# A two-layer trunk on one core: each engine's order tied to the order of the trace, forgetting heads spread over their group, all their probabilities transposed by DMA

## The chip, the cores and the metric

The kernel runs on one core of one Trainium2 chip. TensorE (PE in the profile) multiplies matrices, VectorE (DVE) and ScalarE (ACT) do the elementwise work, GpSimd (POOL) a little of it, and SyncE (SP) issues nearly all transfers. The metric is the device time of one execution in microseconds, as the median of several; less is better. Instructions on one engine run in the order in which they stand in its queue; between engines, semaphores make an instruction wait for what it reads or overwrites.

## The reference

Two layers on a sequence of 256 tokens with 2048 channels. Layer 0 mixes tokens by forgetting attention (16 heads of 128), layer 1 by dilated sliding windows (8 heads in 3 groups, values 256 wide). Each mixer is followed by an MLP with squared ReLU and 8192 hidden channels. All in fp32.

```python
def fox_attention(h, w_in, b_f, q_gain, k_gain, w_out):
    q, k, v, f = jnp.split(h @ w_in, [H * dh, 2 * H * dh, 3 * H * dh], axis=-1)
    q = rms_norm(q.reshape(B, S, H, dh), q_gain)
    k = rms_norm(k.reshape(B, S, H, dh), k_gain)
    c = jnp.cumsum(jax.nn.log_sigmoid(f + b_f), axis=1)
    # per block of 128 query tokens, every head
    s = jnp.einsum('bqhd,bkhd->bhqk', q_i, k) * scale
    s = s + jnp.transpose(c_i, (0, 2, 1))[..., None] - c_keys[:, :, None, :]
    p = jax.nn.softmax(jnp.where(causal, s, -jnp.inf), axis=-1)
    return jnp.einsum('bhqk,bkhd->bqhd', p, v) ... @ w_out

def reference(x, ...):
    for i in range(2):
        h = rms_norm(x, mix_norm_g[i])
        x = x + (fox_attention if i == 0 else dilated_attention)(h, ...)
        h = rms_norm(x, mlp_norm_g[i])
        x = x + sq_relu_mlp(h, mlp_w_up[i], mlp_w_down[i])
    return x
```

## The kernel before, in words

**Products.** All weights are read once from HBM, in an order fixed by a list (`plan`). A chunk is 256 rows by 512 columns (512 KB). `load` brings it into one of five raw buffers through SP's queue. `split` (L302) cuts it into a high part (`wh`, a cast on ACT, L312) and a low part (`wl`, raw minus high on DVE, L313), with five buffers of each. PE multiplies high by high, high by low and low by high, so that the sum is close to fp32. A k-step covers 128 rows of the weights: for each of two token blocks three matmuls of 512 columns (L347 to L349). A chunk lasts two k-steps. After every second k-step `split` is called for the chunk that is five ahead, since one pair of buffers has just come free, and `load` for the raw chunk whose buffer that split frees.

**Ticks.** After each k-step `product_steps` calls `jobs.tick()`. `Jobs` holds generators ("jobs"): a job is run until it yields a number (so many ticks to wait) or a key (wait until some other job has put it into `done`). Everything beside the products is such a job: the norms of queries and keys (`qk_chain`), values (`v_chain`), attention heads, additions to the residual stream. So the place at which an instruction is traced is set by these yields.

**From trace to queue.** The traced instructions are then put in order by a list scheduler of the compiler's, engine by engine. It keeps dependencies, and a few more ties written by hand: `behind(...)` keeps the instructions in it after given ones. In `move`, a DMA stands behind the latest weight load; in `fox_head`, `pv` and `dil_head` the small matmuls stand behind the latest product; in `p_split` and `qk_chain` casts and subtractions stand behind the latest chunk's cast and cut. Besides these ties the scheduler may move an instruction ahead of others traced before it or behind others traced after it.

**Forgetting heads.** The stage makes four groups `j` of four heads. For each, three products of 16 k-steps: queries (`fq`), keys (`fk`), values (`fv`). A group takes 48 ticks; its heads run in the ticks of its last products and of the next group's first. After a product of queries or keys, `qk_chain` norms it, transposes it through DRAM by DMA, and makes two halves of tokens (t = 0, 1) two ticks apart, each scaled and cut in high and low on ACT and DVE; with the second half the key ("fk", j) is done. The first head's scores come two ticks later.

`fox_head` (L739) makes one head:
- the bias row, from DRAM to all partitions (`bias`, 192 KB, through SP, two buffers), four ticks later the mask is added to it (L752, DVE);
- scores on PE (`sc_f`, L666 to L669), for two blocks of 128 queries, then on DVE scores plus bias (`s_f`, L765) and the row maximum (`nm_f`, L768);
- one tick later exp on ACT with the row sums (L771); one tick later on DVE the reciprocal (L774) and the scaling (L776);
- the transposition of the probabilities, in `p_turned` (L613): a 32 by 32 transpose on DVE (L617), four block moves to DRAM (`pblocks`, 48 KB each, SP), four ticks later one read back (`turned`, 192 KB, SP), and five ticks after it `p_split` (L627) makes the high part on ACT (`pTh`, L632) and the low on DVE (`pTl`, L634). In the last group, heads 14 and 15 use `p_transposed` (L637) instead: three PE transposes and copies on ACT and DVE;
- three ticks later `pv` (L597), the product with the values on PE (`po_f`, L606, L607), cut into the operands of the output projection (`oTfh` on ACT, L609; `oTfl` on DVE, L610).

The offset `at` (L741) says how many ticks after ("fk", j) a head's scores come: 2, 6, 10, 14 for the heads of groups 0 to 2; 2, 4, 6, 9 in group 3. The first head asks for its bias early and waits for the keys; the others ask for it `at` - 4 ticks after the keys.

**What follows.** The output projection takes its 16 steps in two parts (`in_pair`): steps 0 to 11 of two column blocks, then 12 to 15 of each, so that heads 12 to 15 are needed 24 ticks after its start. Then the first MLP, the dilated layer with its `dil_head` jobs (of the same kind, three scores each), its projection, and the second MLP. `dilation_tables` makes three tables of 128 by 384 with about 28 short DVE operations; it is spawned after the output projection is traced.

Of the kernel before, what the change touches and what calls it, by code (L numbers as in the profile page):

```python
# [42 lines left out]
class Jobs:  # L43
# [5 lines left out]
    def __init__(self):  # L49
        self.now = 0  # L50
        self.live = []
        self.done = set()
        self.running = False

    def spawn(self, gen):
        self.live.append([self.now, None, gen])
        if not self.running:
            self._run()
# [18 lines left out]
    def tick(self):  # L77
        self.now += 1
        self._run()

    def need(self, key):
        tries = 0
        while key not in self.done:
            self.tick()
            tries += 1
            assert tries < 10000, key
# [3 lines left out]
def trunk(ctx: ExitStack, tc, x, fox_w_in, fox_b_f, fox_q_gain, fox_k_gain, fox_w_out, dil_w_in,  # L90
          dil_q_gain, dil_k_gain, dil_w_out, mix_norm_g, mlp_norm_g, mlp_w_up, mlp_w_down, out):
    nc = tc.nc
    jobs = Jobs()

    const = ctx.enter_context(tc.tile_pool(name="const", bufs=1))
    act = ctx.enter_context(tc.tile_pool(name="act", bufs=1))
# [516 lines left out]
    def p_turned(p, name):  # L613


        turned = work.tile([P, 4, 3, 32], F32, tag="s", name=f"turned_{name}", bufs=S_BUFS)
        nc.vector.transpose(turned.rearrange("p j b r -> p b j r"), p.rearrange("p (b j c) -> p b j c", b=3, c=32))  # L617
        blocks = dram.tile([4, 32, 4, 3 * 32], F32, tag="pblocks", name=f"pblocks_{name}", bufs=4)
        for i in range(4):
            move(blocks[:, :, i, :].rearrange("j c x -> c j x"),  # L620
                 turned[32 * i:32 * i + 32].rearrange("p j b r -> p j (b r)"))
        yield 4
        move(turned.rearrange("p i b r -> p (i b r)"), blocks.rearrange("j c i x -> (j c) (i x)"))
        yield 5
        return turned
# [11 lines left out]
    def p_transposed(p, name):  # L637

        pt = ps_tp.tile([P, 3 * P], F32, tag="tp", name=f"ptp_{name}")
        for b in range(3):  # L640
            nc.tensor.transpose(pt[:, b * P:(b + 1) * P], p[:, b * P:(b + 1) * P], ident)
        p_hi, p_lo = (work.tile([P, S], F32R, tag=f"pT{x}", name=f"pT{x}_{name}", bufs=2) for x in "hl")
        p_whole = work.tile([P, P], F32, tag="s", name=f"pTw_{name}", bufs=S_BUFS)
        nc.scalar.copy(p_hi, pt[:, 0:S])
        nc.vector.tensor_sub(p_lo, pt[:, 0:S], p_hi.bitcast(F32))
        nc.scalar.copy(p_whole, pt[:, S:3 * P])
        return p_hi, p_lo, p_whole
# [90 lines left out]

    def fox_head(j, hh, qT, kT, vt):  # L739
        h = 4 * j + hh  # L740
        at = ((0, 2, 4, 7) if j == 3 else (0, 4, 8, 12))[hh] + 2  # L741
        yield ("fq", j)
        yield "gate"
        yield "mask"
        if hh:
            yield ("fk", j)
            yield at - 4

        bias = work.tile([P, 3 * P], F32, tag="bias", name=f"bias{h}", bufs=2)
        move(bias, negc[h:h + 1, :].to_broadcast([P, 3 * P]))  # L750
        yield 4
        nc.vector.tensor_add(bias, bias, tables["mask"])  # L752
        if hh == 0:
            yield ("fk", j)
            yield 2
        ps = ps_sc.tile([P, 512], F32, tag="sc", name=f"sc_f{h}")
        with behind(issued["product"]):
            for t in range(NT):
                scores(ps, t, qT[hh // 2], kT[hh // 2], hh % 2)
        s = work.tile([P, 3 * P], F32, tag="s", name=f"s_f{h}", bufs=S_BUFS)  # L760
        nm = small.tile([P, NT], F32, tag="nm", name=f"nm_f{h}")
        den = small.tile([P, NT], F32, tag="den", name=f"den_f{h}")
        spans = [slice(0, P), slice(P, 3 * P)]
        for t in range(NT):
            nc.vector.scalar_tensor_tensor(s[:, spans[t]], ps[:, spans[t]], c_q[:, t, h:h + 1],  # L765
                                           bias[:, spans[t]], ALU.add, ALU.add)
        for t in range(NT):
            nc.vector.tensor_reduce(nm[:, t:t + 1], s[:, spans[t]], AX.X, ALU.max, negate=True)  # L768
        yield 1
        for t in range(NT):  # L770
            nc.scalar.activation(s[:, spans[t]], s[:, spans[t]], AF.Exp, bias=nm[:, t:t + 1],  # L771
                                 accum_out=den[:, t:t + 1])
        yield 1
        nc.vector.reciprocal(den, den)  # L774
        for t in range(NT):
            nc.vector.tensor_scalar_mul(s[:, spans[t]], s[:, spans[t]], den[:, t:t + 1])  # L776
        if j == 3 and hh > 1:
            yield 2
            pt_sb = p_transposed(s, f"f{h}")
            yield 1  # L780
        else:
            turned = yield from p_turned(s, f"f{h}")
            yield ("fv", j)
            pt_sb = p_split(turned, f"f{h}")
        yield 3
        if ("f", h // 2) not in oT:
            oT["f", h // 2] = tuple(
                act.tile([P, 2, S], F32R, tag=f"aT{x}", name=f"oTf{x}_{h}", bufs=KC // 2) for x in "hl")
        hi, lo = oT["f", h // 2]
        yield from pv(pt_sb, vt, [hh * P], [hi[:, h % 2, :]], [lo[:, h % 2, :]], f"f{h}")  # L790
        jobs.done.add(("of", h))


    def dil_head(q4, i, qTs, kTs, vt):
        h = 2 * q4 + i
        for g in range(3):
            yield ("dqk", q4, g)
        yield (3 if q4 == 3 else 6) * i + 2
        s = work.tile([P, 3, 3 * P], F32, tag="sd", name=f"sd{h}", bufs=1)
        for g in range(3):  # L800
            yield ("table", g)
            ps = ps_sc.tile([P, 512], F32, tag="sc", name=f"sc_d{h}_{g}")
            with behind(issued["product"]):
                for t in range(NT):
                    scores(ps, t, qTs[g], kTs[g], i)
            slope = 2.0 ** (-8.0 * (g * DH + h + 1) / N_SLOPES)
            nc.vector.scalar_tensor_tensor(s[:, g, :], tables[g], -slope, ps[:, 0:3 * P], ALU.mult, ALU.add)
            yield 1
        nm = small.tile([P, NT], F32, tag="nm", name=f"nm_d{h}")
        den = small.tile([P, NT], F32, tag="den", name=f"den_d{h}")  # L810
        spans = [slice(0, P), slice(P, 3 * P)]
        for t in range(NT):
            nc.vector.tensor_reduce(nm[:, t:t + 1], s[:, :, spans[t]], AX.XY, ALU.max, negate=True)
        yield 1
        for t in range(NT):
            nc.scalar.activation(s[:, :, spans[t]], s[:, :, spans[t]], AF.Exp, bias=nm[:, t:t + 1],
                                 accum_out=den[:, t:t + 1])
        yield 1
        nc.vector.reciprocal(den, den)
        p = work.tile([P, 3 * P], F32, tag="s", name=f"p_d{h}", bufs=S_BUFS)  # L820
        nc.vector.tensor_add(p, s[:, 0, :], s[:, 1, :])
        nc.vector.tensor_add(p, p, s[:, 2, :])
        for t in range(NT):
            nc.vector.tensor_scalar_mul(p[:, spans[t]], p[:, spans[t]], den[:, t:t + 1])
        if (q4, i) == (3, 1):
            yield 2
            pt_sb = p_transposed(p, f"d{h}")
        else:
            turned = yield from p_turned(p, f"d{h}")
            yield ("dv", q4)  # L830
            pt_sb = p_split(turned, f"d{h}")
        yield 3
        hi, lo = (act.tile([P, 2, S], F32R, tag=f"aT{x}", name=f"oTd{x}_{h}", bufs=KC // 2) for x in "hl")
        oT["d", h] = hi, lo
        yield from pv(pt_sb, vt, [i * S, i * S + P], [hi[:, 0, :], hi[:, 1, :]], [lo[:, 0, :], lo[:, 1, :]], f"d{h}")
        jobs.done.add(("od", h))
# [147 lines left out]

    tag = "n0"
    for j in range(4):
        qT = [heads_pair(f"fqT{j}_{i}", i, False) for i in range(2)]
        kT = [heads_pair(f"fkT{j}_{i}", 3 + i, True) for i in range(2)]
        vt = values(f"fv{j}")
        product(keys_h(tag), lhs_h(tag), lambda acc: qk_chain(  # L990
            acc, tag, ("fq", j), [(0, 2, FOX_G, qT[0]), (2 * P, 2, FOX_G, qT[1])]))
        if j == 0:
            jobs.need("wf")
            gate(tag)
        product(keys_h(tag), lhs_h(tag), lambda acc: qk_chain(
            acc, tag, ("fk", j), [(0, 2, FOX_G + 1, kT[0]), (2 * P, 2, FOX_G + 1, kT[1])]))

        for hh in range(4):
            jobs.spawn(fox_head(j, hh, qT, kT, vt))
        product(keys_h(tag), lhs_h(tag), lambda acc: v_chain(acc, tag, ("fv", j), vt))  # L1000
# [42 lines left out]
```

## Time and profile before

| | before |
|---|---|
| three executions | 2166.27, 2163.27, 2166.0 us |
| median | 2166.0 us |
| the profiled execution | 2165.23 us |
| its span, first to last instruction | 2163.5 us |
| mean granted clock of PE | 0.999 |
| PE, DVE, ACT busy share of the span | 99%, 65%, 51% |

The profile is one execution. The forgetting stage runs from about 30 to 330 us, the first MLP to about 1150, the dilated stage to about 1430, the second MLP to the end. In a line of the timeline stand the start, the duration, the engine, the source line, the operation, output and inputs, and in brackets how long the engine was idle before it and what released it. In the groups, "xN" is a count and three durations are the least, the median and the greatest in ns. In the view of waits stand the engine and its instruction, whom it waited for, the total, how many times, and the longest. Matmuls are pipelined: a 512-column one shows 0.38 us, but they start every 0.216 us.

### The profile page before, as it was taken

What the parts mean: (1) busy time and instruction counts of PE and PEld (TensorE: products, weight loads), DVE (VectorE), ACT (ScalarE), POOL (GpSimd) and SP (SyncE); (2) the same over time, 40 slices, a digit from 0 to 9 for tenths busy, and PEclk for the clock granted to TensorE, in tenths of its full rate; (3) what the DMA queues carried; (4) which work ended last, traced back from release to release, by engine and by line L of the source; (5) the groups of instructions that cost most, each with busy time, mean ns of one, the idle gap of its engine ahead of it and who ended that gap; (6) DMA issues with size and microseconds to landing.
All of it is one profiled execution on the core that took longest, in us unless ns stands there. A gap on an engine that the chain in (4) does not pass through costs nothing.

```text
span 2163.5 us, 29880 instructions
## 1 busy us (share of the span) xinstructions
PE 2145.4 (99%) x11129; PEld 1904.4 (88%) x11129; DVE 1409.8 (65%) x1890; ACT 1101.6 (51%) x1524; POOL 41.6 (2%) x40
## 2 busy tenths in 40 slices
PE   9999999999999999999999999999999999999999
PEld 7888888998998998998887888888988988988988
DVE  6778778765665565566668778676755655655664
ACT  6555565644444454455555555545544543544542
POOL 0000000000000000000000000000000000000000
PEclk9999999999999999999999999999999999999999
DMA  7877687766666666667777776758656656656664
GB/s 240 253 240 232 218 274 262 236 202 202 201 204 204 200 201 204 203 200 241 243 239 222 226 243 212 259 198 272 204 203 201 201 204 204 199 203 203 202 212 141
DMA packets 312369, 470.77 MB, mean 218 GB/s; under 512 B 34648, under 2 KB 121888, under 8 KB 312224
## 3 DMA queue, kind: packets, MB, share of 16 engines
q1 hardware_dynamic: 311632, 468.20, 66.8%
q8 instruction: 87, 1.43, 0.3%
q10 hardware_dynamic: 560, 0.66, 0.1%
q14 instruction: 58, 0.48, 0.1%
q0 software_dynamic: 32, 0.02, 0.0%
HBM read 445.76 MB, written 23.03 MB: 217 GB/s over the span
## 4 chain that ended last, share of the span: by engine, by line
PE 89%; DVE 3%; issue 1%; ACT 0%; DMA 0%; POOL 0%; SPq 0%; ACTq 0%; DVEq 0%; POOLq 0%
PE acc L347 19%; PE acc L349 19%; PE acc L348 19%; PE up_n1a_acc L411 5%; PE up_n3a_acc L411 5%; PE up_n1a_sc L411 3%; PE up_n1a_tp L411 3%; PE up_n3a_sc L411 3%; PE up_n3a_tp L411 3%; PE up_n3a_acc L415 3%; PE up_n1a_acc L415 3%; DVE wl L313 1%; PE up_n3a_tp L415 1%; PE up_n3a_sc L415 1%; PE up_n1a_tp L415 1%; PE up_n1a_sc L415 1%
## 5 line engine op out<-in xcount | busy, mean ns | idle before, releaser
L313 DVE TENSOR_TENSOR wl<-raw,wh 128x1024 fp32r<-128x1024 f32 (+1 forms) x801 | 973.8, 1220 | 632.7 <-ACT wh L312 629.3
L312 ACT CAST wh<-raw 128x1024 fp32r<-128x1024 f32 (+1 forms) x801 | 836.5, 1047 | 901.8 <-PE acc L349 553.7
L348 PE MATMUL acc<-wl,hT_n 128*128 128x512 f32 x896 | 341.8, 381 | 1.3 <-DVE wl L313 1.1
L347 PE MATMUL acc<-wh,hT_n 128*128 128x512 f32 x896 | 342.6, 384 | 0.0
L349 PE MATMUL acc<-wh,hT_n 128*128 128x512 f32 x896 | 340.8, 381 | 0.0
L347 PE MATMUL acc<-wh,aTh_n1a 128*128 128x512 f32 x512 | 194.0, 379 | 0.0
L348 PE MATMUL acc<-wl,aTh_n1a 128*128 128x512 f32 x512 | 194.0, 379 | 0.0
L349 PE MATMUL acc<-wh,aTl_n1a 128*128 128x512 f32 x512 | 194.0, 379 | 0.0
L348 PEld LDWEIGHTS acc<-wl,hT_n 128*128 128x128 f32 x896 | 170.3, 190 | 24.8 <-DVE wl L313 2.3
L349 PEld LDWEIGHTS acc<-wh,hT_n 128*128 128x128 f32 x896 | 170.2, 190 | 23.7
L347 PEld LDWEIGHTS acc<-wh,hT_n 128*128 128x128 f32 x896 | 170.2, 190 | 23.2 <-ACT wh L312 0.4
L347 PE MATMUL acc<-wh,aTh_n3a 128*128 128x512 f32 x480 | 181.9, 379 | 0.0
L348 PE MATMUL acc<-wl,aTh_n3a 128*128 128x512 f32 x480 | 181.9, 379 | 0.0
L349 PE MATMUL acc<-wh,aTl_n3a 128*128 128x512 f32 x480 | 181.9, 379 | 0.0
L411 PE MATMUL up_n1a_acc<-hT_n,wh 128*128 128x512 f32 x512 | 181.6, 382 | 0.0
L411 PE MATMUL up_n3a_acc<-hT_n,wh 128*128 128x512 f32 x512 | 181.6, 382 | 0.0
L415 PE MATMUL up_n3a_acc<-hT_n,wl 128*128 128x256 f32 x512 | 139.6, 273 | 0.0
L415 PE MATMUL up_n1a_acc<-hT_n,wl 128*128 128x256 f32 x512 | 139.6, 273 | 0.0
L348 PEld LDWEIGHTS acc<-wl,aTh_n1a 128*128 128x128 f32 x512 | 96.8, 189 | 13.8
L349 PEld LDWEIGHTS acc<-wh,aTl_n1a 128*128 128x128 f32 x512 | 96.8, 189 | 13.7
L347 PEld LDWEIGHTS acc<-wh,aTh_n1a 128*128 128x128 f32 x512 | 96.8, 189 | 13.6
L411 PEld LDWEIGHTS up_n3a_acc<-hT_n,wh 128*128 128x128 f32 x512 | 96.8, 189 | 13.5
(687 smaller groups left out, 3156.6 us busy)
## 6 DMA issues: line engine op xcount, KB each, us to landing
raw<-in_mlp_w_up_dram SPq DMA_DIRECT2D x256, 512.0 KB, 4.3
raw<-in_mlp_w_down_dram SPq DMA_DIRECT2D x256, 512.0 KB, 3.7
raw<-in_dil_w_in_dram SPq DMA_DIRECT2D x192, 256.0 KB, 4.0
raw<-in_fox_w_in_dram SPq DMA_DIRECT2D x95, 512.0 KB, 5.5
raw<-in_fox_w_out_dram SPq DMA_DIRECT2D x32, 512.0 KB, 5.1
raw<-in_dil_w_in_dram SPq DMA_DIRECT2D x32, 512.0 KB, 5.0
raw<-in_dil_w_out_dram SPq DMA_DIRECT2D x32, 512.0 KB, 4.0
blocks_n<-turned_n SPq DMA_DIRECT2D x96, 64.0 KB, 3.2
```

Of the source, the lines that this page charges most:

```text
L312: issued["cast"] = nc.scalar.copy(hi[:, part, :], raw[:, part, :])
L313: issued["cut"] = nc.vector.tensor_sub(lo[:, part, :], raw[:, part, :], hi[:, part, :].bitcast(F32))
L347: nc.tensor.matmul(acc[t], ah[:, tok], hi, start=first, stop=False)
L348: nc.tensor.matmul(acc[t], ah[:, tok], lo, start=False, stop=False)
L349: issued["product"] = nc.tensor.matmul(acc[t], al[:, tok], hi, start=False, stop=last)
L411: issued["product"] = nc.tensor.matmul(banks[b], hi[:, i, col], in_turn(tokens.rearrange("p x s -> p (x s)"), P // 2), start=first, stop=last)
L415: nc.tensor.matmul(banks[b][:, 0:S], lo[:, i, col], in_turn(tokens[:, 0, :], P // 2), start=False, stop=False)
```

## The change

One hook is added to `Jobs`, which runs after every tick. From tick 24 on it runs `pin`, which goes over all instructions traced since the last call and adds to each a dependency on the instruction traced before it on the same engine. The dependency is of a kind that orders and needs no semaphore, so that the scheduler keeps every engine's queue in traced order. The offsets of the heads in groups 0 to 2 become 2, 8, 20, 26 (group 3 keeps 2, 4, 6, 9). Heads 14 and 15 go through `p_turned` and `p_split` like the others, and in the last group `pv` comes two ticks after the split instead of three. In the dilated stage's last group the second head starts five ticks behind the first instead of three.

```diff
@@ class Jobs
+        self.each_step = lambda: None
@@ tick
         self.now += 1
         self._run()
+        self.each_step()
@@ trunk
+    pinned = {"last": None}
+
+    def pin():
+
+        traced = nc.cur_bb.bb.instructions
+        at = len(traced)
+        while at and traced[at - 1] is not pinned["last"]:
+            at -= 1
+        if pinned["last"] is None:
+            at = len(traced)
+        for i in traced[at:]:
+            before = pinned.get(i.engine)
+            if before is not None:
+                tc.add_manual_dep(
+                    i, before.name,
+                    mybir.DependencyInfo(mybir.DependencyClass.NoSync, mybir.DependencyReason.DATA),
+                    reason="in the order of the trace")
+            pinned[i.engine] = i
+        pinned["last"] = traced[-1]
@@ fox_head
-        at = ((0, 2, 4, 7) if j == 3 else (0, 4, 8, 12))[hh] + 2
+        at = ((2, 4, 6, 9) if j == 3 else (2, 8, 20, 26))[hh]
...
-        if j == 3 and hh > 1:
-            yield 2
-            pt_sb = p_transposed(s, f"f{h}")
-            yield 1
-        else:
-            turned = yield from p_turned(s, f"f{h}")
-            yield ("fv", j)
-            pt_sb = p_split(turned, f"f{h}")
-        yield 3
+        turned = yield from p_turned(s, f"f{h}")
+        yield ("fv", j)
+        pt_sb = p_split(turned, f"f{h}")
+        yield 2 if j == 3 else 3
@@ dil_head
-        yield (3 if q4 == 3 else 6) * i + 2
+        yield (5 if q4 == 3 else 6) * i + 2
@@ the four groups of forgetting heads
     for j in range(4):
+        if j == 0:
+            jobs.each_step = lambda: jobs.now >= 24 and pin()
```

## The prediction

> **What bounds the kernel now.** The page's first part is read first, then four stretches side by side (the columns: the stretch and its length, busy us and instructions of PE, weight loads, DVE, ACT, POOL, then the granted clock, the DMA share, GB/s).
>
> ```profile
> PE 2145.4 (99%) x11129; PEld 1904.4 (88%) x11129; DVE 1409.8 (65%) x1890; ACT 1101.6 (51%) x1524; POOL 41.6 (2%) x40
> 30.00:330.00 300.00, 294.92 (x1444) 254.51 (x1443) 229.43 (x419) 173.85 (x301) 15.24 (x11) 1.00 0.75 242
> 330.00:1150.00 820.00, 820.00 (x4295) 732.82 (x4294) 518.41 (x631) 407.16 (x530) 6.30 (x5) 1.00 0.66 214
> 1150.00:1430.00 280.00, 275.39 (x1348) 240.79 (x1347) 210.41 (x318) 159.68 (x243) 16.83 (x9) 0.99 0.72 231
> 1430.00:2159.00 729.00, 729.00 (x3928) 654.55 (x3927) 434.16 (x491) 343.64 (x425) 0.70 (x1) 1.00 0.63 205
> ```
>
> TensorE is the bound: it idles for nothing in either MLP, 300 - 294.9 = 5.1 us in the forgetting stage, 280 - 275.4 = 4.6 us in the dilated one. What PE waits for longest in those two stages:
>
> ```profile
> PE sc_d L666 <- DVE sd L807: 2.3, 2, 2.0
> PE po_f L606 <- DVE s_f L765: 1.9, 1, 1.9
> PE po_d L606 <- DVE pTl_d L634: 1.8, 1, 1.8
> PE po_f L606 <- ACT pTh_f L632: 0.9, 1, 0.9
> ```
>
> So the change can win at most about 10 us by order, while each wait that a fixed order makes is a full loss. The clock of the work is the tick, one k-step of six 512-column products; ACT casts one weight chunk per two ticks:
>
> ```profile
> 1140.06 1.05 ACT L312 CAST wh<-raw 128x1024 fp32r<-128x1024 f32 x1 [1.54 <-PE acc L349]
> 1147.83 1.05 ACT L312 CAST wh<-raw 128x1024 fp32r<-128x1024 f32 x1 [1.54 <-PE acc L349]
> ```
>
> (1147.83 - 1140.06) / 6 = 1.295 us a tick. Each cast starts when PE has left a buffer (the releaser): in traced order ACT and DVE cannot run ahead of PE, and what is traced behind a chunk's cast and cut waits for both. The first forgetting head in the trace of before:
>
> ```profile
> 87.48 0.38 PE L666 MATMUL sc_f<-fkT_0w,fqT_0w 128*128 128x128 f32 x2
> 107.49 0.42 DVE L634 TENSOR_TENSOR pTl_f<-turned_f,pTh_f 128x256 fp32r<-128x256 f32 x1
> 108.52 0.27 PE L606 MATMUL po_f<-pTh_f,fv0h 128*128 128x256 f32 x1
> ```
>
> From its scores to its last operand (107.49 + 0.42) are 20.4 us, and its values product ran 21.0 us after the scores. In traced order that product stands 14 ticks behind them, plus two score groups of other heads (some 0.5 us each): due at 14 x 1.295 + 1.0 = 19.1 us. The scheduler of before had moved it two ticks back.
>
> **The change part by part.** *The pin.* It adds no instruction and no semaphore; it fixes each engine's order to the traced one. In both MLPs the orders of before and after hardly differ: 0, hidden by PE's 100% there; the ring holds five chunks, ten ticks or 13 us ahead. One move into the first MLP counts: about 28 operations for the dilation tables go from the output projection to its start.
>
> ```profile
> L209 DVE TENSOR_TENSOR dist<-dist,ok 128x384 f32<-128x384 f32 x1 | 0.6, 553 | 0.0
> ```
>
> 28 x 0.45 = 12.6 us of DVE in eight ticks, beside four cuts of 1.22 us: DVE falls back at most 7 us, under the 13 us lead. Cost 0; without cover up to 7. The dilated stage keeps its order but for a few moves by one or two ticks: 0, between -4.6 (its idle) and +4.
>
> *The forgetting heads, groups 0 to 2.* Offsets 8, 20, 26 put head 1's scores 6 ticks behind head 0's, head 3's 6 behind head 2's. On SP head 1's bias request now stands behind head 0's four block moves (before: ahead of them), likewise head 3's behind head 2's. Rows for a walk:
>
> ```profile
> 88.92 0.74 DVE L765 SCALAR_TENSOR_TENSOR s_f<-sc_f,c_q,bias 128x128 f32<-128x128 f32 x2 [0.25 <-PE sc_f L669]
> 89.58 1.22 DVE L313 TENSOR_TENSOR wl<-raw,wh 128x1024 fp32r<-128x1024 f32 x1
> 90.71 0.60 DVE L768 TENSOR_REDUCE nm_f<-s_f 128x1 f32<-128x128 f32 x2
> 91.02 0.40 ACT L771 ACTIVATE s_f<-s_f,nm_f 128x128 f32<-128x128 f32 x1 [1.88 <-DVE nm_f L768]
> 91.91 1.03 ACT L312 CAST wh<-raw 128x1024 fp32r<-128x1024 f32 x1
> 92.04 0.17 DVE L774 RECIPROCAL den_f<-den_f 128x2 f32<-128x2 f32 x1 [0.73 <-ACT s_f L771]
> 92.83 0.58 DVE L617 STREAM_TRANSPOSE turned_f<-s_f 128x384 f32<-128x384 f32 x1
> 94.96 1.94 SPq L269 DMA_DIRECT2D pblocks_f<-turned_f  x4
> L752 DVE TENSOR_TENSOR bias<-bias,mask x16: 513/548/559, 80.1 to 317.6; 128x384 f32<-128x384 f32 x16
> DMA to landing us min/median/max: 3.3/4.2/5.6
> pblocks_f<-turned_f SPq DMA_DIRECT2D x56, 48.0 KB, 2.1
> turned_f<-pblocks_f SPq DMA_DIRECT2D x14, 192.0 KB, 5.5
> L632 ACT CAST pTh_f<-turned_f x14: 388/397/408, 106.6 to 326.5; 128x256 fp32r<-128x256 f32 x14
> ```
>
> From the start of head 0's scores: cast to 1.25, cut to 2.5, scores add and maximum (0.74, 0.60) to 3.85, four exp instructions (91.02 to 91.91) to 4.9, next cast to 5.95 and cut to 7.2, since the traced order has them ahead of the reciprocal; reciprocal to transpose (92.04 to 93.4) to 8.6; four moves to 10.4. Then bias 1 is requested: 10.4 + 4.2 = 14.6, and DVE, in order, stands at its mask add till then. Mask add, scores, maximum to 16.5; exp 17.55; cast and cut 19.8; reciprocal to transpose 21.2; cut 22.4; and only then, as DVE's order has it, head 0's last operand (0.42) at 22.8. Due 19.1: **3.6 us**. Head 1: transposed at 21.2, four moves to 23.0, landed at 25.1 (2.1), read back at 30.6 (5.5), split at 31.4 (0.40, 0.42); due 20 ticks and three groups behind head 0's scores, shifted by the wait: 25.9 + 1.5 + 3.6 = 31.0. **0.4**.
>
> Head 2's product comes out later, for two more things stand ahead of its last operand: a projection output's cut and the next projection's sums of squares.
>
> ```profile
> L610 DVE TENSOR_TENSOR oTfl<-po_f,oTfh 128x256 fp32r<-128x256 f32 x16 | 6.5, 413 | 11.0 <-ACT oTfh L609 10.9
> L532 DVE TENSOR_REDUCE ss_('fk', 1)_1429<-sq_('fk', 1)_1_1427 128x4 f32<-128x512 f32 x1 | 0.7, 686 | 0.0
> ```
>
> 22.8 + 0.4 + 1.55 (two sums and a short scaling, taken as the reciprocal's 0.17) = 24.8, against 19.1: 5.7; and ACT may stand at head 1's split till its read has landed, 0 to 2.4 us: half, 1.2. Bias 3 and head 3 hold it as bias 1 and head 1 hold head 0's. Halves of the 1.2 may fall together with DVE's, so 5.7 + 0.6 = **6.3**. The first scores wait for the keys' second half, whose operations stand behind two casts, the first half and both value copies on ACT:
>
> ```profile
> 83.45 0.50 ACT L567 ACTIVATE fkT_0w<-qn_('fk', 0)_0_766,gain 128x256 f32<-128x256 f32 x1
> 85.12 0.69 ACT L586 ACTIVATE fv0w<-acc,rstd_n 128x512 f32<-128x512 f32 x1
> 86.63 0.91 ACT L567 ACTIVATE sq_('fk', 0)_0_715<-qn_('fk', 0)_1_769,gain 128x256 f32<-128x256 f32 x2
> 87.91 0.42 DVE L576 TENSOR_TENSOR fkT_0l<-sq_('fk', 0)_0_715,fkT_0h 128x256 fp32r<-128x256 f32 x1
> ```
>
> Counted from four ticks (5.2 us) before the scores: 2 x 1.05 + 4 x 0.5 + 2 x 0.69 + 0.91 + 2 x 0.42 = 7.2, less some 0.5 by overlap: **1.5** late. Last, a long wait costs the clock:
>
> ```profile
> 1159.00:1162.00 3.00, 1.13 (x6) 0.64 (x4) 3.00 (x6) 1.04 (x1) 0.00 (x0) 1.00 0.66 201
> 1162.00:1166.00 4.00, 3.83 (x13) 3.23 (x14) 3.51 (x6) 0.00 (x0) 0.00 (x0) 0.59 0.62 159
> ```
>
> After one wait of about 2 us PE ran the next 4 us at 0.59: 4 x 0.41 = **1.7** lost, taken once a group. The Trainium skill, TensorE: Matmul & The Clock Gate, Part 1, has the rate halved only after an idle window of about 3.4 us; the row differs, as a shorter wait did it, and by the page's rule the sum would be some 5 us less.
>
> A group: 1.5 + 3.6 + 0.4 + 6.3 + 1.7 = 13.5; three: 40.5.
>
> *Group 3.* Heads 14 and 15 go by DMA: eight moves, two reads and two transposes more, six PE transposes less (6 x 0.109 = 0.7 us at PE's pitch). Four heads stand within 7 ticks; one head's turn on DVE is 0.55 + 0.74 + 0.60 + 1.0 + 1.05 + 1.22 + 1.4 = 6.55 us. Head 12 is transposed at 8.6, head 13 at 15.2, head 14's maximum ends at 17.05. Head 12's read-back stands on SP behind head 13's moves and behind a weight load that waits for the cut after that maximum:
>
> ```profile
> SPq L293 <- DVE wl L313: 45.8, 24, 4.1
> turned_d<-pblocks_d SPq DMA_DIRECT2D x7, 192.0 KB, 2.4
> ```
>
> Load and read are issued at 21, landed at 26.5, split at 27.4; due 13 ticks and four score groups behind the first: 16.8 + 2.0 = 18.8. **8.6** late; with 1.5 for the keys and 1.7 for the clock 11.8. Heads 13 to 15 follow inside that shift: 0. The added transfers' other cost, 2 x 0.57 us on DVE, lies in the same wait.
>
> *Sum.* 40.5 + 11.8 - 5.1 (the waits of before, gone with their order) - 0.7 = 46.5; 2165.2 (the profiled run: span 2163.5 and 1.7 around it) + 46.5 = 2212; that run lies 0.8 under the median of 2166.0.
>
> *Bounds.* With the fastest bias (3.3: 0.9 less), the dilated heads' read (2.4) and no hold on ACT a group is 1.5 + 2.7 + 0 + 4.8 + 1.7 = 10.7 and the last 1.5 + 5.5 + 1.7 = 8.7: 32.1 + 8.7 - 5.8 = +35; without clock losses (-6.8) +28: 2193. With the slowest bias (5.6: 1.4 more), a read 1.1 longer, the full hold and two clock losses a group: 1.5 + 5.0 + 0.4 + 9.5 + 3.4 = 19.8 and 1.5 + 9.7 + 3.4 = 14.6: 59.4 + 14.6 - 5.8 = +68: 2233. A price for the read from the Trainium skill, DMA: Bandwidth & Descriptors, the fit of 2.0 us plus bytes over 436 GB/s, would be 2.45 us as an estimate; the 5.5 of this trace differs, and by the page group 3's term would be about 5.5.
>
> **The rivals.** *Only the last group pays.* If bias 1 lands before DVE reaches it, the pairs close inside their 14 ticks: 4 x 1.5 + 8.6 + 1.7 - 5.8 = +10.5, 2176; half-way cases up to 2192. For it: 20.4 us of before held waits for a bias and slow reads too. Against: the bias now starts behind four moves that wait for a transpose.
>
> *Faster.* PE's waits of before came from a scheduler that placed products early. If the split of a first head ends under 19.1 us (its own chain, with no turn behind head 1, ends at 10.4 + 2.1 + 5.5 + 0.8 = 18.8), fixed places are late enough and nothing waits: -5.1 - 0.7 = -5.8, with the dilated idle up to -10.4: 2155 to 2159. It decides on one point, the bias request landing before DVE's mask add at about 10.5 us after the scores; against it stands 10.4 as the time of the request.
>
> *No effect.* The order that is pinned is near the one that ran, or gains and losses cancel: 2162 to 2170.
>
> *The ring runs dry.* Weight loads stand on SP behind moves that wait for DVE, and DVE falls more than 13 us back: over 2233.
>
> **How the numbers follow.** Forecast 0.55 (own range 2193 to 2233), last group alone 0.21, faster 0.15, no effect 0.05, ring dry 0.04. The range leaves out faster and ring dry: 2162 to 2233. A change under 0.2% (4.3 us) can't be told from none: faster 0.15, within 0.05, slower 0.80.
>
> **What would show it.** In the profile after: PE idle of 45 to 60 us in the forgetting stage; the values products of heads 0 and 2 waiting for DVE's pTl (3 to 8 us each), those of head 12 for the read-back; DVE idle at the mask add of the second and fourth head, ended by the bias DMA; clock dips behind. Wrong if DVE's mask add never waits, or the waits stand in the dilated stage.

## The result and the profile after

| | before | after |
|---|---|---|
| median | 2166.27 us (5 runs, 2163.27 to 2167.86) | 2224.2 us (5 runs, 2222.59 to 2227.96) |
| span of the profiled execution | 2163.5 us | 2222.5 us |
| mean granted clock of PE | 0.999 | 0.990 |

The ratio is 1.027, with a 95% interval from 1.0255 to 1.0285: the changed kernel is 58 us slower.

Where the time went is read first from two marks. The tile view of the up projection of each MLP gives the start of its first and of its last matmul; the two kernels execute the same products between such marks. Before:

```profile
L411 PE MATMUL up_n1a_acc<-hT_n,wh x512: 382/382/382, 380.4 to 963.5; 128*128 128x512 f32 x171
L411 PE MATMUL up_n3a_acc<-hT_n,wh x512: 382/382/382, 1492.8 to 2076.0; 128*128 128x512 f32 x171
```

After:

```profile
L432 PE MATMUL up_n1a_acc<-hT_n,wh x512: 382/382/382, 425.6 to 1009.9; 128*128 128x512 f32 x171
L432 PE MATMUL up_n3a_acc<-hT_n,wh x512: 382/382/382, 1549.2 to 2132.3; 128*128 128x512 f32 x171
```

The first MLP starts 45.2 us later (425.6 - 380.4): that is the forgetting stage with its output projection. Inside that up projection another 1.2 us are lost (1009.9 - 963.5 = 46.4), from there up to the start of the second MLP 10.0 (1549.2 - 1492.8 = 56.4), and to the end 2.6 (2222.5 - 2163.5 = 59.0).

PE's waits after (the engine and its instruction, whom it waited for, total us, times, longest):

```profile
PE po_f L627 <- ACT pTh_f L653: 18.7, 5, 4.8
PE po_f L627 <- DVE pTl_f L655: 14.0, 9, 2.3
PE sc_d L687 <- DVE sd L823: 7.2, 8, 3.2
PE sc_f L690 <- ACT fkT_0h L595: 3.4, 4, 1.5
PE ptp_d L662 <- DVE p_d L840: 3.2, 1, 3.2
...
PE last L410 <- DVE x L883: 2.2, 1, 2.2
...
PE sc_f L690 <- DVE fkT_0l L597: 1.4, 4, 0.4
```

The values products of the forgetting heads wait 32.7 us for the two parts of their probabilities (in before 0.9 and 0.5 us for these, and once 1.9 us for DVE's `s_f`); the first scores wait 4.8 us for the keys. What DVE waits for in the same profile:

```profile
DVE bias L773 <- DMA bias<-negc: 33.5, 7, 6.4
```

In before the tile view of the bias had 0.9 us of it in the same stage. The timelines of the first group show how it comes about. SP after:

```profile
98.65 1.80 SPq L290 DMA_DIRECT2D pblocks_f<-turned_f  x4
100.50 0.45 SPq L290 DMA_DIRECT2D bias<-negc  x1
```

Head 1's bias is requested when head 0's four block moves are through. DVE:

```profile
93.21 0.74 DVE L786 SCALAR_TENSOR_TENSOR s_f<-sc_f,c_q,bias 128x128 f32<-128x128 f32 x2
...
98.05 0.58 DVE L638 STREAM_TRANSPOSE turned_f<-s_f 128x384 f32<-128x384 f32 x1
...
105.30 0.56 DVE L773 TENSOR_TENSOR bias<-bias,mask 128x384 f32<-128x384 f32 x1 [3.69 <-DMA bias<-negc]
...
112.40 0.42 DVE L655 TENSOR_TENSOR pTl_f<-turned_f,pTh_f 128x256 fp32r<-128x256 f32 x1
```

DVE stands 3.69 us at the mask add of head 1, and head 0's last operand, which stands behind head 1's operations in its queue, is ready at 112.82. PE:

```profile
110.16 0.38 PE L627 MATMUL po_f<-pTh_f,fv0h 128*128 128x256 f32 x1
112.87 0.38 PE L627 MATMUL po_f<-pTl_f,fv0h 128*128 128x256 f32 x1 [2.34 <-DVE pTl_f L655]
```

For heads 2 and 3 the same chain passes through ACT. DVE, ACT and PE, one after the other:

```profile
137.37 0.56 DVE L773 TENSOR_TENSOR bias<-bias,mask 128x384 f32<-128x384 f32 x1 [5.19 <-DMA bias<-negc]
```

```profile
139.01 0.40 ACT L792 ACTIVATE s_f<-s_f,nm_f 128x128 f32<-128x128 f32 x1 [9.46 <-DVE nm_f L789]
...
143.72 0.39 ACT L653 CAST pTh_f<-turned_f 128x256 fp32r<-128x256 f32 x1
```

```profile
144.17 0.58 PE L627 MATMUL po_f<-pTh_f,fv0h 128*128 128x256 f32 x1 [4.83 <-ACT pTh_f L653]
146.35 0.58 PE L627 MATMUL po_f<-pTl_f,fv0h 128*128 128x256 f32 x1 [1.59 <-DVE pTl_f L655]
```

ACT stands 9.46 us at head 3's exp, which needs the bias; head 2's cast is queued behind it, and from 139.01 to its start ACT has no idle time.

### The profile page after: what moved, and what is told of

It reads as the page before. It is cut to its first block, busy times and chain, and to the rows that moved or that the text cites. A ratio compares the mean times of both kernels' runs of the same rounds, so it can differ in the third digit from the quotient of the medians.

```text
span 2222.5 us, 29937 instructions
## 1 busy us (share of the span) xinstructions
PE 2161.3 (97%) x11123; PEld 1915.4 (86%) x11123; DVE 1431.6 (64%) x1892; ACT 1089.2 (49%) x1522; POOL 53.0 (2%) x40
## 4 chain that ended last, share of the span: by engine, by line
PE 75%; DVE 3%; DMA 2%; ACT 2%; issue 1%; SPq 1%; POOL 0%; ACTq 0%; DVEq 0%; POOLq 0%
PE acc L369 15%; PE acc L368 15%; PE acc L370 15%; PE up_n3a_acc L432 5%; PE up_n1a_acc L432 5%; PE up_n3a_tp L432 3%; PE up_n3a_sc L432 3%; PE up_n3a_acc L436 3%; PE up_n1a_tp L432 2%; PE up_n1a_acc L436 2%; PE up_n1a_sc L432 2%; DMA raw<-in_dil_w_in_dram 2%; DVE wl L334 1%; PE up_n3a_tp L436 1%; PE up_n3a_sc L436 1%
```

## The experiments

Each ran beside the kernel before on the same chip; ratios are to it. Where a part of the time is named by stage, it is read from the same marks as above. In the diffs, "-" is the changed kernel.

**Which part of the change it is.** First the change without the tie:

```diff
-            jobs.each_step = lambda: jobs.now >= 24 and pin()
+            pass
```

> The change without the tie: spread heads, all probabilities by DMA, the dilated offset, in the scheduler's own order. My theory (the fixed order makes the waits): the forgetting stage idles 5 to 10 us as before, 2160 to 2172 us. Rival (the pairs of heads or the added DMAs make them): waits of 3 to 7 us at the values products stay, over 2195 us.

Measured: 2179.48 us, ratio 1.0065 (1.005 to 1.008). Most of the loss is gone, so the tie is needed for it; but 14 us stay, more than my theory allowed. So the other edits cost something by themselves; by the marks it lies in the forgetting stage (the first MLP starts at 395.1, 14.7 us later than in before).

Then the tie with the old offsets of the forgetting heads and the PE transposes:

```diff
-        at = ((2, 4, 6, 9) if j == 3 else (2, 8, 20, 26))[hh]
+        at = ((0, 2, 4, 7) if j == 3 else (0, 4, 8, 12))[hh] + 2
...
-        turned = yield from p_turned(s, f"f{h}")
-        yield ("fv", j)
-        pt_sb = p_split(turned, f"f{h}")
-        yield 2 if j == 3 else 3
+        if j == 3 and hh > 1:
+            yield 2
+            pt_sb = p_transposed(s, f"f{h}")
+            yield 1
+        else:
+            turned = yield from p_turned(s, f"f{h}")
+            yield ("fv", j)
+            pt_sb = p_split(turned, f"f{h}")
+        yield 3
```

> The tie with the heads' old offsets and the old PE transposes of heads 14 and 15; the dilated offset stays as changed. My theory: four heads 4 ticks apart take DVE 6.55 us each against 5.2 us of ticks, so the tie costs at least as much here, 2200 to 2240 us. Rival (the spread costs, not the tie): 2165 to 2180 us.

Measured: 2201.7 us, ratio 1.0171 (1.0154 to 1.0188), inside the expectation at its lower end. The tie costs 37 us with the old heads as well, 23.0 of them in the forgetting stage; the new places and the two DMA heads make it worse by some 21 us (1.027 less 1.0171, by 2166), they don't cure it. In that kernel DVE waits for a bias only once (5.6 us): a tie with the old places loses along other chains than the one above.

Of the change without the tie, the PE transposes were put back too (the second half of the diff above):

> No tie and the old PE transposes of heads 14 and 15: of the change only the spread of the heads and the dilated offset. The run without the tie lost 14 us, of it about 10 after 300 us. If the two DMA heads cost that: 2167 to 2172 us. If the spread does: 2176 to 2182 us.

Measured: 2173.68 us, ratio 1.0037 (1.0024 to 1.005), between the two. So in the scheduler's own order the spread costs 8 us and the two DMA heads 6 (2179.48 - 2173.68), while each case of the expectation put nearly all on one of them. The dilated offset of 5 stays in this run and costs nothing without the tie: from the last matmul of the first MLP's up projection to the end it takes 1197.7 us, before 1200.0.

**Whose order it is.** The tie on PE alone:

```diff
-            if before is not None:
+            if before is not None and i.engine == mybir.EngineType.PE:
```

> Only PE is tied to the trace; DVE, ACT, POOL and SP go back to the scheduler. My theory (what is queued ahead of a head's operations on DVE, ACT and SP makes them late): most waits go, 2165 to 2185 us. Rival (the values products simply stand too early on PE, whatever the other engines do): waits stay, 2205 to 2225 us.

Measured: 2215.7 us, ratio 1.0235 (1.022 to 1.025): my expectation failed, the rival's number held. All of the loss lies in the forgetting stage (its first MLP starts at 432.3, 51.9 us later than in before). Its waits are those of PE's places again:

```profile
PE po_f L627 <- ACT pTh_f L653: 24.7, 13, 5.1
PE po_f L627 <- DVE pTl_f L655: 12.4, 13, 2.0
```

DVE waits only 1.7 us for biases in it, so the chain is not held by the same thing. With PE's places given, the scheduler orders ACT and DVE so that the split of head 2 again comes behind head 3's exp: one line of ACT's timeline follows the other.

```profile
142.30 0.40 ACT L792 ACTIVATE s_f<-s_f,nm_f 128x128 f32<-128x128 f32 x1 [2.70 <-DVE nm_f L789]
...
143.19 0.39 ACT L653 CAST pTh_f<-turned_f 128x256 fp32r<-128x256 f32 x1
```

And the complement, everything tied but PE:

```diff
-            if before is not None:
+            if before is not None and i.engine != mybir.EngineType.PE:
```

> DVE, ACT, POOL and SP tied, PE left to the scheduler, which now puts head 2's product 3 ticks later, the first scores of groups 1 to 3 two ticks later, others up to 3. My theory (what counts is the distance on PE between scores and product): head 2's waits fall from 7 to about 3 us, the keys' wait of groups 1 to 3 goes, 2185 to 2200 us. Rival (the order on DVE, ACT and SP alone makes the loss): 2212 to 2226 us.

Measured: 2191.61 us, ratio 1.0121 (1.0104 to 1.0138), inside the range of my theory, but not for its reason alone. A free PE takes away 32 us of the 58; by the marks 17.7 of them in the forgetting stage (425.6 - 407.9) and the other 15 behind the first MLP's up projection, where the theory had nothing. What is left in the forgetting stage has changed its form: after head 2 PE waits 2.9 to 4.5 us a group for a weight chunk's cast (queued on ACT behind head 3's exp, for which ACT stood 9.6 us in the first group), no longer for the values product.

**Later places.** The values products of groups 0 to 2 four ticks later in the trace:

```diff
-        yield 2 if j == 3 else 3
+        yield 2 if j == 3 else 7
```

> The change with the values products of groups 0 to 2 four ticks (5.2 us) later in the trace; the bias stays where it is. My theory (the tied place is earlier than the chain of one head can be, by 2.6, 0.7 and 7 us): the waits of heads 0, 1 and 3 go, head 2's falls to about 2, some 10 us a group with the clock: 2190 to 2200 us. Rival (the standstill of DVE and SP itself holds up the weights, so that the waits follow the place): 2212 to 2226 us.

Measured: 2209.48 us, ratio 1.0206 (1.0191 to 1.0221): half of what I expected, and just outside the rival's range. The waits at the products of groups 0 to 2 went (one of 1.4 us was left), but others came in their place:

```profile
PE sc_f L690 <- ACT fkT_0h L595: 8.8, 4, 3.8
PE acc L368 <- ACT wh L333: 6.5, 4, 2.5
```

The second line is the projection itself short of weights. ACT in this run:

```profile
138.56 0.40 ACT L792 ACTIVATE s_f<-s_f,nm_f 128x128 f32<-128x128 f32 x1 [10.01 <-DVE nm_f L789]
...
139.45 1.97 ACT L333 CAST wh<-raw 128x1024 fp32r<-128x1024 f32 x2
```

While ACT stands 10 us at an exp, the casts queued behind it don't run, and the lead of five chunks (13 us) is used up. So the standstill costs by itself, also where the product stands later; my theory for this run had only the product's place in it.

**The bias.** Heads 1 and 3 of groups 0 to 2 ask for it earlier, by `ahead` = 4 ticks in one kernel and 1 in another; the mask add stays where it was:

```diff
         at = ((2, 4, 6, 9) if j == 3 else (2, 8, 20, 26))[hh]
+        ahead = 4 if hh % 2 and j < 3 else 0
...
-            yield at - 4
+            yield at - 4 - ahead
...
-        yield 4
+        yield 4 + ahead
```

> The change with one edit: heads 1 and 3 of groups 0 to 2 ask for their bias four ticks earlier, ahead of the block moves of the head before. My theory (DVE stands 3.7 us at the mask add until the bias lands, and ACT behind it): the wait of head 0's product goes and head 2's falls from 7 us to 0 to 3; 25 to 33 us less than the change with its share of the clock, 2190 to 2200 us. Rival (it is the casts and cuts in line, or the read-back): 2215 to 2225 us.

Measured: 2190.38 us, ratio 1.0119 (1.0104 to 1.0135). With one tick:

> The change with the bias of heads 1 and 3 asked for one tick earlier: just ahead of the four block moves instead of just behind them. If its place behind the moves (which wait for the transpose and take 1.8 us) makes DVE's standstill: about two thirds of the gain of the four-tick edit, 2198 to 2206 us. If the transfer's own 4.8 us is the cause and only a long lead helps: 2215 to 2222 us.

Measured: 2190.37 us, ratio 1.0111 (1.0097 to 1.0124): the whole gain of the four ticks, not two thirds of it. In this kernel SP and DVE read:

```profile
94.02 0.46 SPq L290 DMA_DIRECT2D bias<-negc  x1
97.66 0.37 SPq L314 DMA_DIRECT2D raw<-in_fox_w_in_dram  x1
98.93 1.81 SPq L290 DMA_DIRECT2D pblocks_f<-turned_f  x4
```

```profile
101.82 0.55 DVE L774 TENSOR_TENSOR bias<-bias,mask 128x384 f32<-128x384 f32 x1
```

One tick in the trace moves the request by 6.5 us on the chip (100.50 to 94.02), since it no longer stands behind a weight load that waits for a cut, nor behind four moves that wait for the transpose. The mask add no longer waits. So the place in SP's queue, not the lead in ticks, makes the standstill, and it is worth 34 us of the 58.

**The rest.** The tie ended ahead of the dilated layer:

```diff
+    jobs.each_step = lambda: None
     dilated("n2")
```

> The change, with the tie ending ahead of the dilated layer. My reading of its profile: the dilated stage lost 9 to 10 us more than before and the last product 2.3 us, all to the tie, so 2209 to 2215 us with the dilated stage idle about 5 us. Rival (the dilated offset of 5, or what the forgetting stage leaves behind): 2220 to 2226 us.

Measured: 2208.03 us, ratio 1.0198 (1.0183 to 1.0214). From the ratios, (1.027 - 1.0198) x 2166 = 16 us belong to the tie behind the first MLP, more than the 12.6 that the marks show there (59.0 - 46.4) but with both kernels' intervals of some 3 us. The marks of its own profile are the closer reading: from the last matmul of the first MLP's up projection to the end it takes 1201.1 us, the changed kernel 1212.6 and before 1200.0, so 11.5 us belong to the tie there. The runs above divide them further: with PE alone tied this stretch takes 1201.3 us, with all engines but PE 1197.7. Only both together lose there.

Three edits together (`ahead` = 4, `yield 2 if j == 3 else 5`, the tie's end as above):

> Three edits on the change at once: the bias of heads 1 and 3 four ticks earlier, values products of groups 0 to 2 two ticks later, the tie ending ahead of the dilated layer. With the early bias alone 2190 us; the tie's end took 16 us off, later places should take the 1.2 to 2.0 us that are left at the products. My theory (the losses are separate and add up): 2168 to 2176 us. Rival (they share the same lateness, so that one cure uses up the others): 2182 to 2190 us.

Measured: 2172.02 us, ratio 1.003 (1.0019 to 1.0041). The losses add up; what is left in its forgetting stage is group 3 (4.3 and 1.3 us at head 12's product) and the keys' waits.

The next run drops the tie ahead of group 3 and gives heads 14 and 15 their PE transposes back:

```diff
-            jobs.each_step = lambda: jobs.now >= 24 and pin()
+            jobs.each_step = lambda: 24 <= jobs.now < 190 and pin()
```

with `ahead` = 4, `p_transposed` for heads 14 and 15, and the products of groups 0 to 2 two ticks later (`yield 3 if j == 3 else 5`).

> The tie for groups 0 to 2 alone (it ends before group 3's heads), bias early, products two ticks later, heads 14 and 15 with PE transposes. My theory (with places and bias right a tied group costs only the keys' wait of 1.5 to 2 us, about what the scheduler loses): 2163 to 2171 us. Rival (the tie itself costs several us a group whatever the places): 2175 to 2185 us.

Measured: 2160.7 us (10 runs), ratio 0.9977 (0.9968 to 0.9986). It is faster than both kernels, by 5 us against the one before, and below my expectation. Its view of PE's waits has no values product of a forgetting head left; of the stage there are the keys and the start of the gate:

```profile
PE sc_f L690 <- ACT fkT_0h L595: 2.1, 3, 0.9
...
PE sc_f L690 <- DVE fkT_0l L597: 1.1, 3, 0.4
...
PE pct L753 <- DVE c_q L749: 0.7, 1, 0.7
```

A tie is therefore not a loss in itself: with 16 ticks between scores and product and the bias ahead of the moves this kernel is a little faster than the one in the scheduler's order. Whether the tie gains anything of it, or the places alone would do the same without a tie, was not run.

One more attempt at a gain: before's heads untied, and all engines but PE tied from the dilated layer on.

```diff
-            if before is not None:
+            if before is not None and i.engine != mybir.EngineType.PE:
...
-            jobs.each_step = lambda: jobs.now >= 24 and pin()
+            pass
...
+    jobs.each_step = pin
     dilated("n2")
```

> Before's forgetting stage untied, with its old offsets and PE transposes; DVE, ACT, POOL and SP tied from the dilated layer on, PE not. In the run with all but PE tied the dilated stage lost 5.6 us where before lost 8.7. If that carries over: 2160 to 2164 us, faster than before. If not: 2164 to 2170 us.

Measured: 2165.1 us (11 runs), ratio 0.9998 (0.9989 to 1.0007). No gain: the expectation of a faster kernel failed.

## Why the prediction was right, and where it was not

**The mechanism and the stage.** The forecast was 46.5 us more, all of it in the forgetting stage; the marks show 45.2 there. The cause is the one that was walked: the bias request behind the block moves holds up DVE, and through the fixed order all that stands behind. That the sum fits this closely is partly luck, for the waits came out some 2.5 us less than forecast (43.0 against 45.5) and the clock's loss some 2.4 us more. By terms:

| term, us a group | predicted | measured |
|---|---|---|
| first scores, keys' second half | 1.5 | 2.3 in group 0, 1.4 in the others |
| head 0's product | 3.6 | 2.4 to 3.0 |
| head 1's product | 0.4 | 0.7, 0.7, none |
| head 2's product | 6.3 | 7.1, 7.0, 6.7 |
| head 12's product in group 3 | 8.6 | 6.3 (4.5 + 1.8) |
| clock | 1.7 | 2.5, 1.3, 3.5 (1.7 + 1.8); 1.9 in group 3 |

The measured waits are the gaps between PE's starts beyond the 0.11 or 0.216 us at which its matmuls follow one another, without the clock. Head 0's walk had the bias requested 10.4 us after the scores began and the last operand at 22.8. In the profile the scores start at 88.39 and stop for 1.7 us; counted from 90.1, behind that wait, the request came at 10.4 and the operand at 22.7 (112.82). The mask add started 4.8 us after the request, predicted 4.2. That the place of this request is the cause, not only a companion, is shown by the one-tick run. Head 2's 6.3 is right in size, and its cause is the walked one, but not its path: the sum had it on DVE's queue, with ACT in it only as half of a possible 2.4 us at head 1's split. In the profile the product waits first for ACT's part (4.83 us, ACT having stood at head 3's exp) and then 1.59 for DVE's. So two of the signs that the prediction named did not show: head 2's product waits mostly for ACT's pTh, not DVE's pTl, and PE is idle for 38.4 us from 30 to 360 us (291.65 busy of 330), not for 45 to 60, as a part of the loss is a slower clock.

**Group 3** was 2.3 us too dear. The read-back was issued in the order that was walked, behind a weight load that waits for the cut after head 14's maximum:

```profile
352.56 0.39 SPq L314 DMA_DIRECT2D raw<-in_fox_w_out_dram  x1
352.99 0.47 SPq L290 DMA_DIRECT2D turned_f<-pblocks_f  x1
```

Counted from 333.9, behind the keys' wait, it was issued at 19.1, where 21 had been walked, and its split started 4.2 us later (357.14), where 5.5 were taken for the landing. But the split was not shown to wait for the landing, which the profile does not record: it stands on ACT behind head 15's exp, which the walk did not have ahead of it, and ACT has no idle time between the two.

```profile
355.31 0.40 ACT L792 ACTIVATE s_f<-s_f,nm_f 128x128 f32<-128x128 f32 x1 [3.09 <-DVE nm_f L789]
...
357.14 0.40 ACT L653 CAST pTh_f<-turned_f 128x256 fp32r<-128x256 f32 x1
```

So the term of 8.6 came out near by another last wait than the read-back; which of the two would have ended it alone stays open.

**The clock** lost more than was said, and not once a group. Stretches of the after kernel behind the waits of 2.6 us (head 0, group 0), 3.0 (head 0, group 2) and 7.1 (head 2, group 0); the column before the last two is the granted clock:

```profile
113.00:117.00 4.00, 4.00 (x21) 3.57 (x22) 3.78 (x6) 1.25 (x3) 1.58 (x1) 1.00 0.84 253
275.00:279.00 4.00, 4.00 (x13) 3.39 (x14) 3.75 (x6) 0.48 (x2) 1.60 (x1) 0.57 0.75 227
147.00:152.00 5.00, 5.00 (x14) 4.06 (x14) 4.93 (x10) 0.98 (x2) 0.79 (x1) 0.50 0.90 267
```

The first lost nothing, the second 4 x 0.43 = 1.7, the third 5 x 0.50 = 2.5. Behind head 2's product in groups 1 and 2 and behind head 12's, the same view has 0.67, 0.55 and 0.53 over 4 us (from 228, 309 and 360 us): 1.3, 1.8 and 1.9. Together that is some 9.2 us, where the sum had 4 x 1.7 = 6.8. The rule of the Trainium skill (TensorE: Matmul & The Clock Gate, Part 1) that the prediction set beside it, a rate halved only after an idle window of about 3.4 us, fits the first but not the second. The prediction's price of that rule, some 5 us less, does not follow from its own terms either: the waits of 6.3 and 8.6 us that it forecast are longer than such a window, so that the clock would be lost in every group by the rule as well.

**The step that was mis-sized** is "The dilated stage keeps its order but for a few moves by one or two ticks: 0, between -4.6 (its idle) and +4", with the 0 for both MLPs. They measured 10.0 us from the end of the first MLP's up projection to the start of the second MLP, 1.2 in the first and 2.6 in the second: 13.8, which, less the 1.3 that the forgetting stage came out cheaper, makes the distance from 2212 to 2224. Few lines stand in another order there, and I took few for harmless. The tie moved just those that matter: the three scores of a dilated head share two buffers, so that each waits for DVE's add of an earlier one (7.2 us in all), and in the last pair DVE has, ahead of the probabilities that PE is to transpose, a chunk's cut that waits for its cast, while the cast stands behind the head's exp on ACT:

```profile
1478.14 1.23 DVE L334 TENSOR_TENSOR wl<-raw,wh 128x1024 fp32r<-128x1024 f32 x1 [2.03 <-ACT wh L333]
...
1480.52 0.55 DVE L840 TENSOR_SCALAR p_d<-p_d,den_d 128x128 f32<-128x128 f32 x2
```

```profile
1476.14 0.94 ACT L832 ACTIVATE sd<-sd,nm_d 128x768 f32<-128x768 f32 x1
...
1477.08 1.98 ACT L333 CAST wh<-raw 128x1024 fp32r<-128x1024 f32 x2
```

In before the scheduler had put that cast ahead of the exp:

```profile
1422.05 1.05 ACT L312 CAST wh<-raw 128x1024 fp32r<-128x1024 f32 x1 [2.57 <-PE acc L349]
1423.01 0.61 ACT L816 ACTIVATE sd<-sd,nm_d 128x384 f32<-128x384 f32 x1
```

A part of the 10.0 us is the clock again: behind the wait of 3.2 us for those probabilities PE ran from 1482 to 1486 us at 0.50. That the tie is the cause here is shown by the run in which it ends earlier; that run keeps the dilated offset of 5, so the offset costs at most 1.1 us without the tie. How the 11.5 us divide over the scores, the last pair and the last product, and what the offset does under the tie, was not tried apart.

**The rivals.** "Only the last group pays" fell with the 33.5 us of DVE at the mask add; where its condition was made, in the run with the bias four ticks earlier, the forgetting stage loses 11.4 us (391.8 - 380.4), close to the 10.5 of that rival. "Faster" took the bias ahead of the mask add as the one point of decision; that alone did not do it (2190.38 us). A faster kernel came only with two more ticks, without the tie from group 3 on and with the PE transposes. "The ring runs dry" did not happen in the changed kernel. In two of the experiments PE ran out of weights as soon as it no longer waited for the products (2.1 to 4.5 us a group), by another route than that rival's, ACT's casts and not the loads on SP: the lead of 13 us that the prediction used as cover for cost 0 was nearly spent by ACT's standstill of 9.5 us.

**The price of single edits.** The two heads moved to DMA were taken at -0.7 and a part of group 3's wait. Without the tie they cost 6 us, and the spread, which I had not priced alone, 8 (with the dilated offset).

## What to carry to other kernels

A fixed order turns every wait at the head of a queue into a wait of everything traced behind it; walk each chain that must close by a given instruction along the queues in their order, DMA requests included, and look for a request that stands behind transfers that wait for another chain. The cure can then be one place in one queue, here one tick earlier for a bias, worth 34 us. An engine that stands still is not made harmless by moving its consumer later: the next thing in its queue, here the weight casts, becomes late.

## What was not expected of the hardware

In the profile of the changed kernel a wait of PE of 2.6 us left the clock at 1.00 once and one of 3.0 us brought 0.57 for the next 4 us, while in before a wait of about 2 us had already brought 0.59: the length of the wait alone doesn't tell what the clock will do.

What goes with it can be read from the view of windows in small steps. The halved stretches of the changed kernel's forgetting stage are 141.9 to 152.2, 223.8 to 230.7, 275.0 to 278.4, 305.7 to 312.6 and 357.0 to 363.8 us: each 3.41 us long or two or three times that, and their starts are whole multiples of 3.41 us apart (275.0 - 223.8 = 15 x 3.41, 305.7 - 275.0 = 9 x 3.41). Cut on that grid, the wait of head 0's product falls across two stretches in group 0 and into one in group 2 (the first number behind the comma is PE's busy time):

```profile
107.80:111.20 3.40, 2.73 (x13) 1.92 (x11) 2.25 (x5) 3.40 (x7) 0.00 (x0) 1.00 0.04 5
111.20:114.60 3.40, 1.73 (x10) 1.60 (x11) 3.40 (x6) 2.31 (x4) 0.00 (x0) 1.00 0.81 217
271.60:275.00 3.40, 0.83 (x4) 0.34 (x3) 3.33 (x8) 3.40 (x6) 0.00 (x0) 1.00 0.47 142
275.00:278.40 3.40, 3.40 (x11) 2.86 (x12) 3.37 (x6) 0.48 (x2) 1.00 (x1) 0.50 0.70 198
```

In the traces of these kernels cut in the same way from 60 to 2100 us (the last run has no halved stretch there and is left out), every full-speed stretch in which PE was busy for 1.42 us or less is followed by a halved one (before, 1159.3: 1.37), and none with 1.65 us or more is; between the two values both occur. This is a reading of the traces; no run was made to test it.
